# The last layer's output projection: transfers in program order, four weight blocks in other buffers, and weight blocks scaled one block earlier

## The chip, the cores and the metric

The kernel runs on one core of a Trainium2 chip. TensorE (PE; its weight loads are shown as PEld), VectorE (DVE), ScalarE (ACT) and GpSimd (POOL) each work through their own instructions in order; SyncE (SP) here only issues transfers (DMA). The metric is the device time of one execution in microseconds (us), as the median of several runs.

## The reference

One inference step of an encoder trunk of two layers, with D = 1024, on 512 prompt tokens and 32 sample tokens, 544 columns in all. In each layer

```python
h = rmsnorm(x, norm_w)
mix, qm, gate = split(h @ w_in)
out = concat([mixer(mix), mem_attention(qm)]) * silu(gate)     # 2048 wide
x = x + out @ w_out                                            # 2048 x 1024
```

Layer 0's mixer is RWKV-7. Layer 1's is differential attention with 12 heads: for each head two softmaxes over two halves of 64 of the keys, one subtracted from the other with a factor, times the values. A final RMSNorm gives the outputs. Layer 1's keys and values, of prompt and sample, are outputs too. All in fp32; the kernel multiplies operands split in a high and a low part, three products for each pair.

## The kernel before

A class `Trunk` writes out the whole program. Each engine stands behind a `Queue` object: `te` (TensorE), `ve` (VectorE), `ae` (ScalarE), `se` (SyncE's transfers), `ge` (POOL). All their instructions are recorded on one line, L132, so the names of tiles tell them apart in the profile. `tie` (L149) can chain the instructions of a queue in the order in which the program writes them (`self.ordered`); otherwise the framework's scheduler and its waits for buffers set the order on that queue.

*The stream of layer 1* (`stream`). The input projection is 56 weight blocks of 1024x128: for each head its values, keys and queries, then gates and memory queries. A block is 48 matmuls ("steps") of 128x272, 2 halves of the columns, 8 pieces of the inner dimension, 3 products. `h` is the normalized activation in f16, high and low (tiles `hh`, `hl`). While a block is multiplied, other work is laid into its steps by small tables:

- `LOADS1`: two loads of 256 KB bring the fp32 weights of the fourth block ahead into one of four slots (`self.raws`, in the profile `h16s`).
- `STAT1` and `SPREAD1`: ScalarE squares a block three ahead (`junkw`); TensorE totals the squares of a block two ahead (a matmul of 128x1).
- `SCALE1`: VectorE makes a power of two from that total, the scale `s` of the block two ahead (`scales`, `power`).
- `SPLITS1`: the next block is split to f16 tiles `whs`, in six pieces: ScalarE twice writes the high part from the raw weights times `s`, POOL twice multiplies the raw weights by `s` in place (`TENSOR_SCALAR h16s<-h16s`), POOL twice subtracts (`TENSOR_TENSOR whs<-h16s,whs`), which gives the low part.

At the start of each q block the head's keys are split too: ScalarE rounds them (`kh`), POOL takes the low part twice (`kz<-k,kh`), and a transfer `kh<-kh` moves rows. Later steps interleave the head's scores (`ps_s`), softmax and products with the values. At the entry to the stream the first two blocks are measured and scaled at once (`measured`).

*The output projection of layer 1* (`w_out`). 16 blocks of `w_out[1]`, each 1024x128: 8 output columns k, two halves q of the 2048 inputs. Here the operands are fp32r in two parts: `whi` and `wlo` from tiles `raw` (half a block each, `RAWS` = 5 of them), and `hi` and `lo` from the 16 gated branch outputs `og0` to `og15`. The first five blocks are loaded by the end of the stream, by `load_steps` into `raw` tiles, or right after it. The order is (0,0), (1,0), then (0,1), (1,1), then k = 2 to 7; the halves q = 1 use the tiles in the order 12 to 15, 8 to 11. After each block `used` splits the next one and loads another. Split blocks have two buffers each for `whi` and `wlo` and a third pair in a pool `fin` (`self.third`). For each finished half of a column `consume` adds the residual x; from k = 2 it also issues, at the second half of a column (`v.start`), one of six entries of `kv_out`: two transfers that copy keys or values from scratch in DRAM to the outputs (`out_dram<-scr`, 1024 KB and 64 KB). `last` makes the final norm.

SyncE's queue is not tied, so these copies can be issued earlier than the code that writes them stands.

## Time and profile before

| | |
|---|---|
| median of 3 runs | 1378.25 us (1376.0 to 1379.12) |
| profiled execution | 1375.76 us |
| its span in the trace | 1374.0 us |
| mean granted clock of TensorE | 0.987 |
| the stream of layer 1, in the trace | 829 to 1246 us |
| the output projection and the final norm | 1246 to 1374 us |
| busy, TensorE / VectorE / ScalarE / POOL | 95% / 67% / 63% / 46% |

Times in the trace count from the span's start. A row of a timeline gives start, duration, engine, operation, tile written `<-` tiles read, partitions x elements, and in brackets how long the engine was idle before it and which engine's work on which tile ended that idle time. Rows of waits give us in total, number of waits, and the longest.

### The profile page before, as it was taken

Reading aid. Unit: us, or ns where it says so; the run is one execution under the profiler, and the core shown is the slowest. Engines: PE = TensorE matmul, PEld = TensorE weight load, DVE = VectorE, ACT = ScalarE, POOL = GpSimd, SP = SyncE. Lnnn points to the kernel's source line nnn. Section 1 sums busy time; section 2 is a strip of 40 time slices with the busy share of each in tenths; the row PEclk is TensorE's granted clock in tenths of the full one; section 3 lists DMA queues with packets and bytes.
Section 4 is the critical chain, followed back from the end, with each engine's and each line's share of the span. In section 5 each row is a group of like instructions: output and inputs, shape, how many; then the busy total and the mean of one; then the engine's idle time right before and its main releaser. Section 6 shows DMA issues by size and latency. Waiting matters only on the chain. (4 is left out here: it accounts for less than half of the span.)

```text
span 1374.0 us, 32094 instructions
## 1 busy us (share of the span) xinstructions
PE 1304.3 (95%) x11713; PEld 1191.3 (87%) x11713; DVE 923.5 (67%) x2391; ACT 865.0 (63%) x2316; POOL 626.0 (46%) x1103
## 2 busy tenths in 40 slices
PE   6999899999999999899999999999999998998797
PEld 6998799999999999888899997888778887888797
DVE  7776667877787777756674473666796668766343
ACT  7665677677767776655644356777767776773221
POOL 2326675558555855560130037656555655561000
PEclk9999999999999999999999999999999999999899
DMA  7542223322332233224275445777767768766421
GB/s 243 171 135 64 56 66 86 88 72 65 83 89 72 64 83 82 75 78 125 72 234 168 128 143 143 193 164 164 162 155 170 164 140 198 159 155 218 131 70 65
DMA packets 418296, 171.53 MB, mean 125 GB/s; under 512 B 195209, under 2 KB 402578, under 8 KB 418138
## 3 DMA queue, kind: packets, MB, share of 16 engines
q1 hardware_dynamic: 417994, 168.96, 47.3%
q8 instruction: 92, 1.51, 0.5%
q14 instruction: 66, 0.54, 0.1%
q10 hardware_dynamic: 144, 0.52, 0.1%
HBM read 130.84 MB, written 41.92 MB: 126 GB/s over the span
## 5 line engine op out<-in xcount | busy, mean ns | idle before, releaser
L132 PE MATMUL ps_g<-h,whs 128*128 128x272 f16 x2688 | 334.8, 280 | 12.5 <-POOL whs L132 12.5
L132 PEld LDWEIGHTS <-whs 128*128 128x128 f16 x2688 | 254.4, 98 | 67.6 <-POOL whs L132 15.8
L132 PE MATMUL ps_g<-hl,whi 128*128 128x272 f32 x976 | 283.9, 297 | 0.5 <-POOL hl L583 0.5
L132 PE MATMUL ps_g<-hh,wlo 128*128 128x272 f32 x912 | 277.2, 304 | 1.3 <-DVE wlo L132 1.3
L132 PE MATMUL ps_g<-hh,whi 128*128 128x272 f32 x912 | 274.4, 301 | 0.9 <-ACT hh L132 0.9
L872 POOL TENSOR_TENSOR tm<-u,m 102x84 f32<-102x84 f32 (+23 forms) x372 | 155.4, 418 | 164.8 <-DMA m<-sc 134.2
L132 DVE TENSOR_TENSOR wlo<-raw,whi 128x512 fp32r<-128x512 f32 x208 | 149.7, 735 | 83.8 <-ACT whi L132 81.8
L132 ACT CAST whi<-raw 128x512 fp32r<-128x512 f32 x210 | 125.3, 616 | 97.0 <-PE ps_g L132 45.2
L132 PEld LDWEIGHTS ps_g<-hl,whi 128*128 128x128 f32 x976 | 183.7, 190 | 2.4 <-POOL hl L583 0.7
L132 PEld LDWEIGHTS ps_g<-hh,whi 128*128 128x128 f32 x912 | 174.3, 191 | 4.4 <-ACT hh L132 1.3
L132 PEld LDWEIGHTS ps_g<-hh,wlo 128*128 128x128 f32 x912 | 173.9, 191 | 4.7 <-DVE wlo L132 2.1
L874 POOL TENSOR_TENSOR u<-u,tm 102x84 f32<-102x84 f32 (+23 forms) x372 | 161.0, 433 | 29.1
L132 PE MATMUL ps_g<-hi,whi 128*128 128x272 f32 x448 | 130.5, 292 | 10.5 <-ACT hi L132 10.5
L132 POOL TENSOR_SCALAR h16s<-h16s 128x512 f32<-128x512 f32 x112 | 78.9, 716 | 125.6 <-ACT whs L132 118.2
L132 PE MATMUL ps_g<-lo,whi 128*128 128x272 f32 x448 | 130.5, 291 | 0.9 <-DVE lo L132 0.9
L132 PE MATMUL ps_g<-hi,wlo 128*128 128x272 f32 x448 | 130.1, 291 | 0.2 <-DVE wlo L132 0.2
L132 POOL TENSOR_TENSOR whs<-h16s,whs 128x512 f16<-128x512 f32 x112 | 128.7, 1169 | 0.2
L132 PEld LDWEIGHTS ps_g<-hi,whi 128*128 128x128 f32 x448 | 85.4, 191 | 11.0 <-ACT hi L132 10.8
L132 PEld LDWEIGHTS ps_g<-lo,whi 128*128 128x128 f32 x448 | 85.3, 190 | 1.6 <-DVE lo L132 1.6
L132 PEld LDWEIGHTS ps_g<-hi,wlo 128*128 128x128 f32 x448 | 85.3, 190 | 0.4 <-DVE wlo L132 0.4
L132 ACT ACTIVATE whs<-h16s 128x512 f16<-128x512 f32 x112 | 74.9, 715 | 6.0 <-DVE h16s L132 4.8
L132 DVE SCALAR_TENSOR_TENSOR SB<-ps_c,dl,sd 64x64 f32<-64x64 f32 x168 | 47.4, 282 | 44.6 <-PE ps_c L132 40.5
(419 smaller groups left out, 2834.1 us busy)
## 6 DMA issues: line engine op xcount, KB each, us to landing
raw<-in_rw_in_dram SPq DMA_DIRECT2D x114, 256.0 KB
h16s<-in_df_in_dram SPq DMA_DIRECT2D x112, 256.0 KB
raw<-in_w_out_dram SPq DMA_DIRECT2D x64, 256.0 KB
ptr<-pk SPq DMA_DIRECT2D x44, 160.0 KB
aT<-ptr SPq DMA_DIRECT2D x11, 640.0 KB
scr<-sg SPq DMA_DIRECT2D x96, 68.0 KB
out_dram<-scr SPq DMA_DIRECT2D x6, 1024.0 KB
m<-sc SPq DMA_DIRECT2D x36, 128.0 KB
```

What stands on the lines that cost most here:

```text
L132: return lambda *a, **k: self.trunk.tie(self, issue(*a, **k))
L872: nc.gpsimd.tensor_tensor(tm[:, :n, :wd], u3[:, :n, kx : kx + 1].to_broadcast(sh), m3[:, kx : kx + 1, kx + 1 :].to_broadcast(sh), ALU.mult)
L874: nc.gpsimd.tensor_tensor(u3[:, :n, kx + 1 :], u3[:, :n, kx + 1 :], tm[:, :n, :wd], ALU.add)
```

## The change

1. The tables: the split of a block has four pieces (steps 2, 5, 8, 11), not six. POOL's scaling in place goes to a new function `scaled`, called at steps 37 and 41 of the block before the one in which the block is split; the scale itself is made at step 32 (`POWER1`), not 36, and the total at step 12, not 20. ScalarE then copies the scaled weights to f16 and no longer multiplies.
2. From the output projection on, the transfers of SyncE's queue are tied to program order (`self.tied = self.se`), and `used` loads a block only when fewer than two are waiting.
3. The blocks of `w_out[1]` that are loaded during the stream go to the four slots of the stream, not to `raw` tiles, and there are four of them.
4. The third pair of split buffers is one tile `w3` in the space of the f16 activations, which are not read any more then; so the pool that holds them (`hctx`) is closed only at the end.
5. `consume` issues a pair of copies at both halves of the columns 2, 3 and 4.

```diff
-LOADS1, SPLITS1 = (1, 14), (2, 5, 7, 9, 12, 15)
-STAT1, SPREAD1, SCALE1 = (11, 27), 20, 36
+LOADS1, SPLITS1 = (1, 14), (2, 5, 8, 11)
+STAT1, SPREAD1, POWER1, SCALE1 = (14, 27), 12, 32, (37, 41)
...
-        if self.ordered:
+        if self.ordered or self.tied is queue:
...
+    def scaled(self, rec, q):
+
+        x = rec["raw"][:, q * KT // 2 : (q + 1) * KT // 2]
+        self.ge.tensor_scalar(x, x, rec["s"], 1.0, ALU.mult, ALU.mult)
...
             self.scales(rec)
+            for q in range(2):
+                self.scaled(rec, q)
...
-        todo = [(lambda k=k: self.ae.activation(hi[:, k], raw[:, k], AF.Copy, scale=s), 0.0) for k in ks]
-        todo += [(lambda k=k: gp.tensor_scalar(raw[:, k], raw[:, k], s, 1.0, ALU.mult, ALU.mult), 0.0) for k in ks]
+        todo = [(lambda k=k: self.ae.copy(hi[:, k], raw[:, k]), 0.0) for k in ks]
         todo += [(lambda k=k: gp.tensor_tensor(lo[:, k], raw[:, k], hi[:, k], ALU.subtract), 0.0) for k in ks]
...
-        if self.ahead:
+        if self.ahead and (self.tied is None or len(self.early) < 2):
             self.early.append(self.load(*self.ahead.pop(0)))
...
-        p, n = (self.third, 1) if third else (self.wp, 2)
-        hi = p.tile([P, KT, P], F32R, tag="whi", name="whi", bufs=n)
-        lo = p.tile([P, KT, P], F32R, tag="wlo", name="wlo", bufs=n)
+        if third:
+            both = self.third.tile([P, 2, KT, P], F32R, tag="hl", name="w3")
+            hi, lo = both[:, 0], both[:, 1]
+        else:
+            hi, lo = (self.wp.tile([P, KT, P], F32R, tag=x, name=x, bufs=2) for x in ("whi", "wlo"))
...
-            self.hctx.close()
             p = self.pool("fin", 1, ctx=ctx, side="right")
-            self.third, self.turn = p, 2
+            self.third, self.turn, self.tied = self.h0, 2, self.se
...
-                if k >= 2 and v.start and kv_out:
+                if k >= 2 and kv_out:
                     kv_out.pop(0)()
...
-            raws = self.load_steps(*self.ahead.pop(0)) if len(self.early) < (3 if isinstance(self.early[0], dict) else 2) else iter(())
+            raws = self.load_steps(*self.ahead.pop(0)) if len(self.early) < 3 else iter(())
...
-                if i == SCALE1 and self.rec is not None:
+                if i == POWER1 and self.rec is not None:
                     self.scales(self.rec)
+                if i in SCALE1 and self.rec is not None:
+                    self.scaled(self.rec, SCALE1.index(i))
...
+        block = self.raws[self.nscaled % 4]
+        self.nscaled += 1
         for q in range(2):
-            raw = self.wp.tile([P, h, P], F32, tag="raw", name="raw", bufs=RAWS)
-            self.se.dma_start(raw[:], src[q * h * P : (q + 1) * h * P, c0 : c0 + P].rearrange("(k p) c -> p k c", p=P))
+            raw = block[:, q * h : q * h + h]
+            self.se.dma_start(raw, src[q * h * P : (q + 1) * h * P, c0 : c0 + P].rearrange("(k p) c -> p k c", p=P))
```

SyncE's queue at the end of the stream and in the output projection, before (`scr` is scratch in DRAM that holds keys and values, `vt`, `vs` and `aT` belong to the attention):

```order
L132 DMA raw<-in_w_out_dram 128x4x128 x7
L132 DMA out_dram<-scr_12356 512x512
L132 DMA out_dram<-scr_12356 32x512
L132 DMA out_dram<-scr_12357 512x512
L132 DMA out_dram<-scr_12357 32x512
L132 DMA out_dram<-scr_14346 512x512
L132 DMA out_dram<-scr_14346 32x512
L132 DMA out_dram<-scr_14347 512x512
L132 DMA out_dram<-scr_14347 32x512
L132 DMA out_dram<-scr_16419 512x512
L132 DMA out_dram<-scr_16419 32x512
```

The same place after:

```order
L132 DMA h16s<-in_w_out_dram 128x4x128 x6
L132 DMA raw<-in_w_out_dram 128x4x128 x12
L132 DMA out_dram<-scr_12360 512x512
L132 DMA out_dram<-scr_12360 32x512
L132 DMA raw<-in_w_out_dram 128x4x128 x2
L132 DMA out_dram<-scr_12361 512x512
L132 DMA out_dram<-scr_12361 32x512
L132 DMA raw<-in_w_out_dram 128x4x128 x2
L132 DMA out_dram<-scr_14348 512x512
L132 DMA out_dram<-scr_14348 32x512
```

Before, nine half blocks stand ahead of all twelve copies, and the second half of the fifth block behind them, with the other 22 loads; after, twenty half blocks stand ahead of the first copy, and each pair of copies is followed by one block.

POOL's queue around a q block of the first heads, before (`kz` is the low part of the keys; the row of scales behind it belongs to the same block as the row of subtractions behind it):

```order
L132 TENSOR_SCALAR h16s<-h16s 128x512 x2
L132 TENSOR_TENSOR whs<-h16s,whs 128x512 x2
L132 TENSOR_TENSOR kz_12351<-k,kh 64x544 x2
L132 TENSOR_SCALAR h16s<-h16s 128x512 x2
L132 TENSOR_TENSOR whs<-h16s,whs 128x512 x2
```

After:

```order
L132 TENSOR_TENSOR whs<-h16s,whs 128x512 x2
L132 TENSOR_SCALAR h16s<-h16s 128x512 x2
L132 TENSOR_TENSOR kz_12355<-k,kh 64x544 x2
L132 TENSOR_TENSOR whs<-h16s,whs 128x512 x2
L132 TENSOR_SCALAR h16s<-h16s 128x512 x2
```

The scales of the block that is split at the q block have moved from behind `kz` to in front of it; the subtractions follow `kz` directly.

ScalarE's queue at the end of the stream, before (`og_12337` to `og_12340` are the branch outputs 12 to 15, `hi` their high parts, `fw` the final norm's weights):

```order
L132 ACTIVATE osT<-ps_osT,dv 128x128
L132 CAST hi_18532<-og_12337 128x544
L132 CAST hi_18534<-og_12338 128x544
L1830 DMA fw<-in_final_norm_w_dram 128x1024
L132 CAST whi<-raw 128x512 x4
L132 CAST hi_18536<-og_12339 128x544
L132 CAST whi<-raw 128x512
L132 CAST hi_18538<-og_12340 128x544
```

After (`og_12341` to `og_12344` are the branch outputs 12 to 15, `w_18582` is the third buffer):

```order
L132 ACTIVATE osT<-ps_osT,dv 128x128
L132 CAST w_18582<-h16s 128x512 x2
L1837 DMA fw<-in_final_norm_w_dram 128x1024
L132 CAST whi<-h16s 128x512 x2
L132 CAST hi_18526<-og_12341 128x544
L132 CAST hi_18528<-og_12342 128x544
L132 CAST hi_18530<-og_12343 128x544
L132 CAST whi<-raw 128x512 x2
L132 CAST hi_18532<-og_12344 128x544
```

The casts of outputs 12 and 13 now follow two weight blocks, and that of output 15 follows the cast of a whole block from `raw` tiles, where it followed one half block.

## The prediction

> **What bounds the kernel now.** I read the busy times first, then TensorE's waits over the whole run, then the chain of work that ended last in the final stage, and last the two stretches to which these lead.

> ```profile
> span 1374.0 us, 32094 instructions
> PE 1304.3 (95%) x11713; PEld 1191.3 (87%) x11713; DVE 923.5 (67%) x2391; ACT 865.0 (63%) x2316; POOL 626.0 (46%) x1103
> ```

> TensorE (PE) is busy 95% of the span, and no matmul is removed. The kernel can gain only from TensorE's idle time and from time at a lower clock. Four rows of TensorE's waits bear on code that the change touches (us in total, times, longest us):

> ```profile
> PE ps_g L132 <- POOL whs L132: 12.5, 11, 2.3
> PE ps_g L132 <- ACT hi L132: 10.5, 1, 10.5
> PE ps_s L132 <- DMA kh<-kh: 2.0, 1, 2.0
> PE ps_g L132 <- DVE lo L132: 0.9, 2, 0.7
> ```

> The first is the weight stream of layer 1, eleven short waits for the low part of a weight block. The second is one wait in the output projection. The chain in the last stage (start, us, what) says what that one wait really was:

> ```profile
> 1256.59 16.38 DMA out_dram<-scr
> 1273.03 4.97 DMA raw<-in_w_out_dram
> 1278.02 0.73 DVE lo L132
> 1278.80 31.62 PE ps_g L132 x233
> ...
> 1315.14 30.68 PE ps_g L132 x245
> ```

> TensorE waits for activations (`hi`), but the chain goes behind them to a weight load, and behind that to the copies of keys and values to the outputs. ScalarE (ACT), SyncE's queue (SPq) and TensorE at that place:

> ```profile
> 1242.33 6.88 SPq L132 DMA_DIRECT2D raw<-in_w_out_dram  x4
> 1249.26 17.66 SPq L132 DMA_DIRECT2D out_dram<-scr  x12
> 1267.01 65.44 SPq L132 DMA_DIRECT2D raw<-in_w_out_dram  x23
> 1276.76 0.62 ACT L132 CAST whi<-raw 128x512 fp32r<-128x512 f32 x1 [14.42 <-DMA raw<-in_w_out_dram]
> 1277.29 1.73 ACT L132 CAST hi<-og 128x544 fp32r<-128x544 f32 x3
> 1277.98 0.59 PE L132 MATMUL ps_g<-hi,whi 128*128 128x272 f32 x1 [10.54 <-ACT hi L132]
> 1278.80 0.59 PE L132 MATMUL ps_g<-lo,whi 128*128 128x272 f32 x1 [0.22 <-DVE lo L132]
> ```

> All twelve copies are issued in a row, and the load after them is the second half of the fifth weight block. Its cast sits on ScalarE for 14.42 us, and the three casts of `hi` that TensorE needs are queued behind it. Windows (us, busy time and count of PE, PEld, DVE, ACT, POOL, then granted clock, DMA share, GB/s) give the price:

> ```profile
> 1265.00:1285.00 20.00, 9.23 (x53) 8.71 (x52) 4.76 (x8) 4.05 (x8) 0.00 (x0) 0.66 0.70 222
> 1315.00:1345.00 30.00, 30.00 (x242) 30.00 (x241) 10.71 (x20) 7.24 (x14) 0.00 (x0) 1.00 0.16 46
> 1136.90:1140.40 3.50, 3.50 (x20) 2.34 (x19) 3.26 (x10) 2.19 (x9) 2.86 (x3) 0.51 1.04 289
> ```

> In the chain above, 245 matmuls take 30.68 us, 0.1252 each. The 20 us from 1265 hold 53 of them, worth 6.6 us, so 13.4 us are lost: 10.54 + 0.22 of waiting, and 2.6 more, since the granted clock is only 0.66 there.

> [...]

> **The change, part by part.** *Copies and loads in program order.* SyncE now issues four whole blocks in the stream and six more ahead of the first copy; then one pair of copies (1024 and 64 KB), two half loads, and so on. The fifth block no longer stands behind a copy, so the wait of 10.54 us goes, with the 0.22 and the clock loss. Late next is the cast of `hi` for tile 15: it now follows the cast of another weight block on ScalarE, whose buffer TensorE must free. Such a cast takes 0.62 us; I estimate 0.5 us of waiting. The gain is 13.4 − 0.5 = 12.9. Its bounds are 13.4 (no new wait) and 10.0 (the wait is 0.8 and is enough to keep the clock low, 2.6).

> The twelve copies go to output columns 2 to 4, two pairs per column. A column is 96 matmuls, 96 × 0.1252 = 12.0 us. The DMA view of 1249 to 1273 gives what copies cost:

> ```profile
> DMA packets 4747, 7.60 MB, mean 317 GB/s; under 512 B 226, under 2 KB 1487, under 8 KB 4746
> out_dram<-scr SPq DMA_DIRECT2D x6, 1024.0 KB
> out_dram<-scr SPq DMA_DIRECT2D x6, 64.0 KB
> ```

> Two pairs are 2.23 MB, and two weight blocks 1.05 MB; at 317 GB/s that is 7.0 + 3.3 = 10.3 us of the column's 12.0. Before, this stage moves 46 GB/s, so there is room, and a load is issued about a column ahead of its split. Cost: 0, hidden by 12 us of matmuls; if that cover fails it is rival C.

> *POOL's scaling moved to the block before.* At a q block TensorE waits like this (POOL, ScalarE, TensorE):

> ```profile
> 939.85 2.75 POOL L132 TENSOR_TENSOR kz<-k,kh 64x544 fp32r<-64x544 f32 x2 [5.09 <-ACT kh L132]
> 940.59 1.33 ACT L132 ACTIVATE whs<-h16s 128x512 f16<-128x512 f32 x2
> 942.70 1.36 POOL L132 TENSOR_SCALAR h16s<-h16s 128x512 f32<-128x512 f32 x2
> 944.02 2.27 POOL L132 TENSOR_TENSOR whs<-h16s,whs 128x512 f16<-128x512 f32 x2
> 945.23 1.33 PE L132 MATMUL ps_g<-h,whs 128*128 128x272 f16 x10 [0.81 <-POOL whs L132]
> ```

> `kz` holds POOL for 2.75 us, the scale for 1.36, and only then come the subtractions, whose first half TensorE awaits. The high part is ready at 941.92, before `kz` ends, so POOL alone is late. With the scale done in the block before, the subtraction starts right after `kz`, 1.36 us sooner. The eleven waits:

> ```profile
> 829.05 0.64 PE L132 MATMUL ps_g<-h,whs 128*128 128x272 f16 x4 [1.49 <-POOL whs L132]
> 1022.06 1.10 PE L132 MATMUL ps_g<-h,whs 128*128 128x272 f16 x8 [2.28 <-POOL whs L132]
> 1165.73 1.10 PE L132 MATMUL ps_g<-h,whs 128*128 128x272 f16 x8 [1.50 <-POOL whs L132]
> 1211.52 0.87 PE L132 MATMUL ps_g<-h,whs 128*128 128x272 f16 x6 [1.22 <-POOL whs L132]
> ```

> The other seven lie between 0.81 (the row at 945.23) and 1.22. The eight up to 1.22 sum to 12.5 − 1.49 − 2.28 − 1.50 = 7.2 and vanish, since each is under 1.36; 1.50 falls to 0.14 and 2.28 to 0.92, another 2.7. The first (1.49) is the entry to layer 1, where the scales now stand on POOL ahead of the last two splits of the activations; it may grow, by 0.4 as I estimate (half of one scale, 0.7, rounded up). So 7.2 + 2.7 − 0.4 = 9.5.

> Three things take some back. Where VectorE (DVE) is nearly full, TensorE would run into it:

> ```profile
> 981.00:1026.00 45.00, 41.44 (x360) 33.84 (x358) 41.03 (x104) 30.17 (x77) 27.09 (x28) 1.00 0.73 176
> 1018.79 1.11 SPq L132 DMA_DIRECT2D kh<-kh  x2
> 1023.58 0.31 PE L132 MATMUL ps_s<-kh,qp 128*128 128x128 f32 x1
> ```

> VectorE is busy 41.03 of 45 us there, and the waits in this stretch give up about 2.5 of the 9.5; I take 1.5 of it as lost. The scores at 1023.58 need the move of `kh` issued at 1018.79 to 1019.90, so 3.7 us later; scores that come 1.36 sooner may wait for it, as they did elsewhere for 2.0: 0.5. And ScalarE's cast now needs POOL's scale first. That wait is new. Today the order is the other way round:

> ```profile
> L132 POOL TENSOR_SCALAR h16s<-h16s 128x512 f32<-128x512 f32 x112 | 78.9, 716 | 125.6 <-ACT whs L132 118.2
> L132 ACT ACTIVATE whs<-h16s 128x512 f16<-128x512 f32 x112 | 74.9, 715 | 6.0 <-DVE h16s L132 4.8
> ```

> POOL idles 118.2 us in front of its scales, so it has room to do them sooner, at steps 37 and 41 of the block before, where no cast is pending. ScalarE's cast follows at steps 2 and 5, some thirteen matmuls after the first scale. If the scale is still behind something, the cast waits at most one scale, 0.72 us. Bounds: 0 if never, 12 × 0.72 = 8.6 if in each of the twelve q blocks and if TensorE feels all of it; nearest is the row of 6.0 us, ScalarE's waits today in front of these casts, nearly all off TensorE's path: 0.5. The stream gains 9.5 − 1.5 − 0.5 − 0.5 = 7.0, with bounds of 0.9 (9.5 − 8.6) and 12.5 (all of the row).

> *Edits at no cost.* The total of squares (a 128x1 matmul pair) moves from step 20 to 12, within the same TensorE work. The third split buffer moves to the space of the activations, free when the stream's last matmul ends. The cast without a scale operand has the same size. The gate on loads (fewer than two waiting) only spaces them; the 12 us column covers it.

> **Sum.** 12.9 + 7.0 = 19.9. Against the profiled execution of 1375.76 us that gives 1355.9; its span of 1374.0 lies 1.8 lower. The median of the runs, 1378.25, is 2.5 above that execution, so for the median I say 1378.25 − 19.9 = 1358.3, rounded to 1358.

> **Rivals.** *A, both parts work:* 1358, by the bounds of small costs 1352 (25.9 gained, every wait gone) to 1362.

> *B, only the output projection pays:* the stream's waits come back as waits for VectorE, for `kh` or for POOL's scale. For it speaks VectorE at 41.03 of 45 us; against it that most of the eleven waits end on POOL with the high part long ready. 1378.25 − 12.9 = 1365.

> *C, the copies now delay the weights:* copies and loads share SyncE's queue, so each column's loads run behind two pairs of copies. At the 222 GB/s of the window from 1265, 3.28 MB need 14.8 us, 2.8 more than a column. Three columns are 8.4, and three clock drops at about 1.7 (half of the 3.5 us at 0.51) 5.1: the 13.5 undo the output part, 1378.25 − 7.0 + 0.6 ≈ 1372. It decides below 3.28 MB / 12.0 us = 273 GB/s. Against it: 317 was measured with the same copies, and the lead of a column is 12 us.

> [...]

> *D, slower:* the new wait of ScalarE for POOL's scale. ScalarE works in order, so a cast that waits holds the exponentials and evacuations behind it, which TensorE needs. If it cost 0.72 us in each of the 56 blocks it would be 40: 1378.25 − 19.9 + 40 ≈ 1398. It decides from 19.9 / 0.72 = 28 blocks on. Against it: POOL has those 118.2 us of idling.

> That the change does not reorder the transfers is excluded by SyncE's order of instructions.

> **Chances.** A 0.64, B 0.20, C 0.09, D 0.04; 0.03 for gains lost in waits that I do not see. The predicted time is A's. The range reaches from A's best, 1351 with the spread of the runs, over B's 1365 and half way to C: 1351 to 1370. Faster by over 0.2% (2.75 us, about what a measurement of this kernel can tell from no change) are A, B and C: 0.93; the same 0.03; slower 0.04.

> **What would show it.** In the changed profile: no wait of TensorE for `hi` of more than 1 us near 1267, a granted clock of 1 through the output projection, copies spread over columns 2 to 4 with loads of `raw` between them and no wait of TensorE for `whi` or `wlo` there; TensorE's waits for POOL `whs` down from 12.5 to about 3 us; POOL's 118.2 us of waiting for ScalarE gone, and in its place waits of ScalarE's `whs` for POOL `h16s`, small. It would be wrong if those last are many and long (D), if new waits on `ps_s` appear beside `kh` or VectorE (B), or if `raw` lands late in columns 3 to 5 (C).

## The result, and the profile after

The changed kernel takes 1358.47 us (median of 4 runs, 1353.73 to 1360.9), the kernel before 1378.68 (4 runs) on the same chip: a ratio of 0.9852, 95% interval 0.9819 to 0.9884, so 20 us less (16 to 25). Forecast were 1358 and 19.9 us less. The sum was right; one of its terms was not, as the runs below show.

The profiled execution is the slowest of the four, 1360.9 us. Its page begins:

```profile
span 1359.1 us, 32016 instructions
PE 1304.9 (96%) x11713; PEld 1192.7 (88%) x11713; DVE 922.2 (68%) x2391; ACT 856.3 (63%) x2316; POOL 630.8 (46%) x1103
```

TensorE does the same work in a span 14.9 us shorter; this is less than the 20 us of the medians because the execution profiled before, of 1375.76 us, was faster than the four runs compared here, and this one is the slowest of its four. Of its waits over the whole run, these are in the code that was changed:

```profile
PE ps_g L132 <- POOL whs L132: 3.6, 2, 2.9
PE ps_s L132 <- DMA kh<-kh: 2.9, 2, 2.2
...
PE ps_mo L132 <- DVE og L132: 1.4, 2, 1.0
PE ps_s L132 <- DVE og L132: 1.3, 1, 1.3
PE ps_aT L132 <- DVE pt L132: 1.3, 1, 1.3
...
PE ps_o L132 <- DMA aT<-ptr: 0.6, 1, 0.6
```

The wait of 10.5 us for `hi` is gone. The eleven waits for POOL have become two. In their place stand short waits for VectorE, for `kh` and for `aT`, of which the kernel before had one for `kh`, of 2.0 us, and one for VectorE, of 0.2 us. In front of its scales POOL no longer waits for ScalarE, 118.2 us before, but for VectorE, which makes the scale:

```profile
L132 POOL TENSOR_SCALAR h16s<-h16s 128x512 f32<-128x512 f32 x112 | 79.1, 719 | 89.0 <-DVE h16s L132 83.0 <-PE ps_o L132 2.1 <-PE ps_g L132 2.0
```

The queues of SyncE and of ScalarE in the output projection:

```profile
1231.00 48.31 SPq L132 DMA_DIRECT2D raw<-in_w_out_dram  x12
1279.35 1.25 SPq L132 DMA_DIRECT2D out_dram<-scr  x2
1280.71 4.66 SPq L132 DMA_DIRECT2D raw<-in_w_out_dram  x2
1285.42 1.18 SPq L132 DMA_DIRECT2D out_dram<-scr  x2
...
1256.56 1.15 ACT L132 CAST whi<-h16s 128x512 fp32r<-128x512 f32 x2 [8.33 <-PE ps_g L132]
1257.60 1.74 ACT L132 CAST hi<-og 128x544 fp32r<-128x544 f32 x3
1259.52 1.15 ACT L132 CAST whi<-raw 128x512 fp32r<-128x512 f32 x2 [0.18 <-PE ps_g L132]
1260.57 2.84 ACT L132 CAST hi<-og 128x544 fp32r<-128x544 f32 x5
```

Copies now come in pairs, 6 to 8 us apart. The weight cast in front of output 15 waits only 0.18 us for a buffer, and output 15 itself (the first of the five casts at 1260.57) is done ahead of its matmuls, so the 0.5 us that the forecast put there are not felt. Two windows (us, busy time and count of PE, PEld, DVE, ACT, POOL, granted clock, DMA share, GB/s): the first is the one in which 13.4 us were lost before, the second holds the copies.

```profile
1265.00:1285.00 20.00, 20.00 (x162) 20.00 (x161) 8.26 (x17) 6.54 (x14) 0.00 (x0) 1.00 0.42 130
1279.00:1315.00 36.00, 36.00 (x291) 35.85 (x291) 15.19 (x28) 8.00 (x16) 0.00 (x0) 1.00 0.77 251
```

From the last matmul of the stream to the end it was 127.8 us before (1246.20 to 1374.04) and is 114.0 now (1245.14 to 1359.09): 13.9 of the 14.9 us. The stream, from its first to its last matmul, went from 419.0 to 416.6 in this execution, only 2.4 shorter where 7.0 were forecast; what stands ahead of the stream was 1.4 longer in it. That gap is what most of the runs are about.

### The profile page after: what moved, and what is told of

It is laid out like the page before. It is cut to its first block, busy times and chain, and to the rows that moved or that the text cites. A ratio compares the mean times of both kernels' runs of the same rounds, so it can differ in the third digit from the quotient of the medians.

```text
span 1359.1 us, 32016 instructions
## 1 busy us (share of the span) xinstructions
PE 1304.9 (96%) x11713; PEld 1192.7 (88%) x11713; DVE 922.2 (68%) x2391; ACT 856.3 (63%) x2316; POOL 630.8 (46%) x1103
## 5 line engine op out<-in xcount | busy, mean ns | idle before, releaser
L132 PE MATMUL ps_g<-h,whs 128*128 128x272 f16 x2688 | 334.1, 281 | 3.6 <-POOL whs L132 3.6
L132 PEld LDWEIGHTS <-whs 128*128 128x128 f16 x2688 | 256.9, 98 | 57.7 <-POOL whs L132 5.3
L132 PE MATMUL ps_g<-hl,whi 128*128 128x272 f32 x960 | 281.5, 298 | 0.6 <-POOL hl L591 0.5
L132 PE MATMUL ps_g<-hh,wlo 128*128 128x272 f32 x912 | 277.9, 305 | 1.3 <-DVE wlo L132 1.3
L132 PE MATMUL ps_g<-hh,whi 128*128 128x272 f32 x912 | 275.1, 302 | 0.9 <-ACT hh L132 0.9
L132 DVE TENSOR_TENSOR wlo<-raw,whi 128x512 fp32r<-128x512 f32 x194 | 140.8, 739 | 64.6 <-ACT whi L132 63.4
L132 PEld LDWEIGHTS ps_g<-hl,whi 128*128 128x128 f32 x960 | 181.6, 191 | 2.4 <-POOL hl L591 0.7
L132 PEld LDWEIGHTS ps_g<-hh,whi 128*128 128x128 f32 x912 | 174.8, 192 | 4.4 <-ACT hh L132 1.3
L132 PEld LDWEIGHTS ps_g<-hh,wlo 128*128 128x128 f32 x912 | 174.3, 191 | 4.8 <-DVE wlo L132 2.1
L132 POOL TENSOR_TENSOR whs<-h16s,whs 128x512 f16<-128x512 f32 x112 | 130.7, 1187 | 51.4 <-ACT whs L132 49.7
L132 ACT CAST whi<-raw 128x512 fp32r<-128x512 f32 x194 | 116.2, 616 | 58.1 <-PE ps_g L132 31.0
L132 POOL TENSOR_SCALAR h16s<-h16s 128x512 f32<-128x512 f32 x112 | 79.1, 719 | 89.0 <-DVE h16s L132 83.0
L132 PE MATMUL ps_g<-hi,whi 128*128 128x272 f32 x384 | 110.7, 288 | 0.9 <-ACT whi L132 0.9
L132 PE MATMUL ps_g<-lo,whi 128*128 128x272 f32 x384 | 110.7, 288 | 0.7 <-DVE lo L132 0.7
L132 PE MATMUL ps_g<-hi,wlo 128*128 128x272 f32 x384 | 110.6, 288 | 0.2 <-DVE wlo L132 0.2
L132 DVE SCALAR_TENSOR_TENSOR SB<-ps_c,dl,sd 64x64 f32<-64x64 f32 x168 | 47.4, 282 | 43.5 <-PE ps_c L132 39.1
L132 PEld LDWEIGHTS ps_g<-hi,whi 128*128 128x128 f32 x384 | 72.2, 188 | 1.2 <-ACT whi L132 1.2
L132 PEld LDWEIGHTS ps_g<-lo,whi 128*128 128x128 f32 x384 | 72.2, 188 | 1.1 <-DVE lo L132 1.1
L132 PEld LDWEIGHTS ps_g<-hi,wlo 128*128 128x128 f32 x384 | 72.3, 188 | 0.4 <-DVE wlo L132 0.4
L132 ACT CAST whs<-h16s 128x512 f16<-128x512 f32 x112 | 65.4, 619 | 9.5 <-POOL h16s L132 7.7
## 6 DMA issues: line engine op xcount, KB each, us to landing
out_dram<-scr SPq DMA_DIRECT2D x6, 1024.0 KB
```

What stands on the lines that cost most here:

```text
L132: return lambda *a, **k: self.trunk.tie(self, issue(*a, **k))
```

## The experiments

Ratios are against the kernel before on the same chip in the same session, whose medians were 1374.3 to 1375.4 us.

**Each part alone.** The first run keeps the old tables, `split_scaled` and `measured`, the second the old output projection.

> The output projection's part alone (transfers in program order, four blocks in the stream's slots, copies two pairs a column); the splits of the stream stand as before. If the two parts add: 12.9 to 13.9 us under before, about 1365, no wait of TensorE for hi near 1267, its waits for POOL whs still about 12.5 us. Rival (the stream's part brings nothing, the rest of the 20 us is in the output projection too): about 1359.

Measured: 0.9897 (0.9873 to 0.9920), 1361.1 us, 13.2 under before.

> The stream's part alone (POOL's scale one block earlier); the output projection as before, so the wait of 10.5 us for hi stays. By the prediction 7.0 us under before, about 1371.5. Rival, from one profiled execution of the changed kernel, whose stream is only 2.4 us shorter (waits for POOL whs 8.9 us less, but 4.9 of other waits and one half-clock stretch at the entry more): about 1376, not to be told from before.

Measured: 0.9961 (0.9945 to 0.9977), 1369.6 us, 4.7 under before. TensorE's waits, in the output part alone and then in the stream's part alone:

```profile
PE ps_g L132 <- POOL whs L132: 12.7, 11, 2.3
PE ps_s L132 <- DMA kh<-kh: 2.3, 2, 2.1
```

```profile
PE ps_g L132 <- ACT hi L132: 10.2, 1, 10.2
PE ps_g L132 <- POOL whs L132: 3.6, 2, 2.9
PE ps_s L132 <- DMA kh<-kh: 2.8, 3, 1.5
PE ps_mo L132 <- DVE og L132: 1.4, 2, 1.0
PE ps_aT L132 <- DVE pt L132: 1.3, 1, 1.3
```

Each part removes its own wait and leaves the other's. They add within the scatter: 1.03% and 0.39% make 1.42%, against 1.48% and, in a second measurement, 1.42% for both; by medians 13.2 and 4.7 make 17.9 us, against 20.2 and 19.2. In the trace of the stream's part the stream takes 413.0 us, 6.0 less than before, and its waits sum to 9.1 us against 15.1: the same 6.0, with one half clock in each (a granted clock of 0.79 from 829 to 837 in the part alone, of 0.51 from 1136.90 to 1140.40 before). So waits explain that trace. The stream differs from one execution to the next: with the changed tables of steps it took 416.6, 413.0, 413.0, 412.1 and 415.9 us in five traces, 414.1 on average, against an average of 419.4 in the four traces with the old tables. That is 5.3 us less.

**What removes the stall: program order or more blocks ahead?** One run takes program order away from the changed kernel, one gives it alone to the kernel before, one drops the copies from the kernel before (four outputs are then not written).

```diff
-        if self.ordered or self.tied is queue:
+        if self.ordered:
```

> The changed kernel without program order on SyncE's queue; four blocks in the stream's slots, the gate on loads and two pairs a column stay in the code, but all twelve copies are again issued in a row, now behind 13 half blocks instead of 9. Theory (program order is what takes the stall away): the 14th half block lands late and TensorE waits some 5 us or more, 1365 or above. Rival (it is enough that more blocks are ahead of the copies): a block is 48 matmuls, 6.0 us, so the seventh is needed 36 us after the stage begins, about 1281 in the trace; the copies have landed by about 1273 and the load 5 us later, so no wait over 1 us and a time within 2 us of the changed kernel.

```diff
-        if self.ordered:
+        if self.ordered or self.tied is queue:
...
-            self.third, self.turn = p, 2
+            self.third, self.turn, self.tied = p, 2, self.se
```

> The kernel before with one thing of the change: SyncE's transfers in program order from the output projection on (no more blocks in the stream, no third buffer moved, copies at the second half of a column, stream as before). All loads of the first ten blocks then stand ahead of the copies. Theory (any order that takes the loads of the fifth to seventh block out from behind the copies does): the 10.5 us for hi are gone, 10 to 13 us under before, unless the last copies, now among the final stores, end later than the norm. Rival (the four blocks in the stream's slots are needed): a wait of several us stays near 1267.

```diff
-                if k >= 2 and v.start and kv_out:
-                    kv_out.pop(0)()
```

> The kernel before without the twelve copies of keys and values, so these four outputs aren't written. Theory (the stall is the copies in front of a load): the wait for hi is gone and so is the half clock, 13 us under before. Rival (the buffers are what is late, for which the copies only fill the time): the wait stays above 3 us.

Measured: 0.9848 (0.9824 to 0.9873) without program order, as the whole change; 0.9888 (0.9869 to 0.9906) with program order alone, as the output part alone; 0.9899 (0.9877 to 0.9921) without copies, the same again. SyncE's queue without program order, then with program order alone:

```profile
1226.20 3.12 SPq L132 DMA_DIRECT2D raw<-in_w_out_dram  x5
1229.37 14.66 SPq L132 DMA_DIRECT2D out_dram<-scr  x12
1256.26 56.59 SPq L132 DMA_DIRECT2D raw<-in_w_out_dram  x19
```

```profile
1239.60 44.07 SPq L132 DMA_DIRECT2D raw<-in_w_out_dram  x17
1283.72 1.26 SPq L132 DMA_DIRECT2D out_dram<-scr  x2
```

In the first, all copies are again in a row in front of nineteen loads, and nothing waits: six and a half blocks are ahead of them. The copies were the cause of the stall, and either half of the cure is enough. How many blocks must stand ahead of the copies was not tried between four and a half, which stall, and six and a half, which do not.

**What do the copies cost now?** The changed kernel without them (the same four outputs not written).

> The changed kernel without the twelve copies of keys and values, so these four outputs aren't written. Theory (a column's 12.0 us hide two pairs of copies and two blocks): the same time as the changed kernel within 1 us, 0.985 of before. Rival (copies still delay weights or the final stores): 2 us or more under the changed kernel, 0.983 or less.

Measured: 0.9856 (0.9837 to 0.9876), against 0.9858 (0.9839 to 0.9878) of the changed kernel in its second measurement, below. They cost nothing that these runs can tell, whose intervals reach some 2.7 us to either side.

**The entry to the stream.** The first wait for POOL grew from 1.49 to 2.86 us. TensorE and POOL there, in the changed kernel:

```profile
831.78 0.64 PE L132 MATMUL ps_g<-h,whs 128*128 128x272 f16 x3 [2.86 <-POOL whs L132]
...
822.77 1.79 POOL L132 TENSOR_SCALAR h16s<-h16s 128x512 f32<-128x512 f32 x2
824.53 1.66 POOL L1753 TENSOR_TENSOR h<-hn,h 128x544 f16<-128x544 f32 x1
826.17 1.36 POOL L132 TENSOR_SCALAR h16s<-h16s 128x512 f32<-128x512 f32 x2
827.51 1.22 POOL L1753 TENSOR_TENSOR h<-hn,h 128x544 f16<-128x544 f32 x1
```

Two blocks are scaled in front of the last two splits of the activations `h`, and POOL has been working without a pause since 821. In the first run below VectorE scales the first block and POOL the second only behind the first block's split, which leaves the second block's split unscaled, so it tells of the wait and is no version to use; in the next VectorE scales both, and POOL the third.

```diff
-            for q in range(2):
-                self.scaled(rec, q)
+            if rec["n"] < 2:                # first run: == 0
+                self.ve.tensor_scalar(rec["raw"], rec["raw"], rec["s"], None, ALU.mult)
+            else:
+                self.pend.append(rec)       # scaled by POOL in stream, behind the first block's split
...
```

> The changed kernel, but at the entry to layer 1 VectorE scales the first block, and POOL scales the second only after the first block's split, so that no scale stands ahead of the last two splits of the activations on POOL. Theory: the first wait, 2.86 us in the changed kernel against 1.49 before, falls to 1.5 or less, and the half clock behind it (3.4 us, worth 1.7) goes: 3 us under the changed kernel, about 1355.5. Rival (the scales aren't what POOL is late with): the wait stays over 2.5 and the time about 1358.5.

> As in the run on the entry, with both first blocks scaled by VectorE and the third by POOL after the first split. Theory: as there, no wait for POOL whs at the first block and no half clock behind it, 3 us under the changed kernel, 0.982 of before. Rival (the time in that run came from the late scale of the second block): the wait comes back and 0.985 of before.

Measured: 0.9841 (0.9815 to 0.9866) and 0.9833 (0.9809 to 0.9857). In the second the only wait for POOL left is the one inside a q block:

```profile
PE ps_s L132 <- DMA kh<-kh: 1.6, 2, 1.0
PE ps_o L132 <- DMA aT<-ptr: 1.5, 1, 1.5
...
PE ps_st L132 <- ACT junkw L132: 0.9, 2, 0.4
...
PE ps_g L132 <- POOL whs L132: 0.7, 1, 0.7
```

The wait at the entry and the half clock behind it are gone (from 829 to 837 the granted clock is 1.00, where the changed kernel has 0.79), and the stream takes 410.6 and 409.5 us. A part of that is only moved: two waits for ScalarE's squares (`junkw`), 0.9 us in all, now stand just ahead of the stream's first matmul, where the changed kernel has none. So scales ahead of the splits of `h` were what made POOL late. By medians the second is 1351.3 us; that it beats the changed kernel is likely from the trace, but the intervals overlap.

**The slower rival.**

```diff
-STAT1, SPREAD1, POWER1, SCALE1 = (14, 27), 12, 32, (37, 41)
+STAT1, SPREAD1, POWER1, SCALE1 = (14, 27), 12, 36, (45, 46)
```

> The changed kernel with the power of two at step 36 and POOL's scales at steps 45 and 46 instead of 37 and 41, so that ScalarE's casts at steps 2 and 5 follow closely. For the slower rival of the prediction (the new wait of ScalarE for POOL): ScalarE's waits for POOL h16s, 7.7 us in the changed kernel, go to 20 us or more, and if TensorE feels them the kernel is 5 us or more over the changed one. Theory (TensorE does not feel waits of ScalarE under a scale's 0.72 us, since a block has 7 us of slack in ScalarE's work): the waits grow, the time stays within 2.5 us of the changed kernel.

Measured: 0.9862 (0.9842 to 0.9881), the time of the changed kernel. ScalarE's waits for the scale, in the changed kernel and in this one:

```profile
ACT whs L132 <- POOL h16s L132: 7.7, 11, 2.6
```

```profile
ACT whs L132 <- POOL h16s L132: 10.7, 9, 3.3
```

They grow by 3.0 us, not to the 20 that the rival named, and TensorE does not feel them. The 7 us of slack in the expectation are no idle time of ScalarE, which in the changed kernel is busy 289 of the 417 us from 829 to 1246, some 2.3 us idle for each of the 56 blocks; they are about one block's length, by which the splits run ahead. The intervals leave room for some 2.7 us either way. So the margin is not that narrow; how late the scale must be to cost time was not found.

**Moving `kh` off SyncE's queue**, tried for a faster version, on the kernel with both first blocks scaled by VectorE:

```diff
-                self.se.dma_start(st["kh"][rows[1 - m], m, :].bitcast(F32), ...)
+                self.ae.dma_start(st["kh"][rows[1 - m], m, :].bitcast(F32), ...)
```

> As the run with both first blocks scaled by VectorE, and the 24 moves of kh are issued by ScalarE, not on SyncE's queue, where the one at 1130.34 in the changed kernel stands behind four stores and a load. Theory (scores wait for kh because SyncE issues it late): the waits of ps_s for kh, 2.9 us in the changed kernel, and the half clock that sometimes follows near 1135 go, 1 to 4 us under that run, 0.981 of before. Rival (24 issues of some 0.4 us on ScalarE and their waits push back its exponentials): no gain, or 2 us more.

Measured: 1.0015 (1.0002 to 1.0029), 1377.9 us, some 25 us over the same kernel with `kh` on SyncE (0.9833). Neither theory said that much. The scores' waits for `kh` are indeed gone; but TensorE's and SyncE's waits have these rows:

```profile
PE ps_o L132 <- DMA aT<-ptr: 22.9, 8, 6.0
...
SPq L132 <- DMA kh<-kh: 49.5, 13, 5.7
```

SyncE now stops thirteen times until a move of `kh`, issued by ScalarE, has landed, and `aT`, which the products with the values need, is issued late. ScalarE's exponentials (`pt`) are not what fell behind: TensorE waits 0.7 us for them in all. In the traces of the kernels before and after, the landings of all transfers are counted on eight semaphores, some 2080 to 2160 landings on each; and with `kh` on SyncE's own queue, in the run with both first blocks scaled by VectorE, SyncE's waits in the stream have no row for `kh`. That the moves hold up SyncE because both queues share these semaphores is my reading and was not shown; a version with a semaphore of their own was not tried.

**The changed kernel once more, and the last candidate.**

> The changed kernel unchanged, on the chip of the next run, for a second trace of it. If its first trace was typical, the stream is again 416 to 417 us and its waits 11 us; if that trace had a stray wait and a stray half clock, as the stream's part alone (413.0) suggests, about 413, the wait of 2.9 us at the entry and the half clock behind it stay, and the time is 0.985 of before.

> Both first blocks scaled by VectorE, four blocks in the stream's slots, and no program order on SyncE's queue. Theory (program order changes nothing once four blocks are in the slots, and the entry is worth 3 us): 3 us under the changed kernel on this chip, 0.983 of before. Rival (the entry's gain is within the scatter): the same as the changed kernel.

Measured: 0.9858 (0.9839 to 0.9878), 1356.2 us, and 0.9842 (0.9818 to 0.9866), 1354.0 us. Of the two cases in the expectation for the changed kernel the first held: its stream took 415.9, not about 413, again with a half clock at the entry (a granted clock of 0.79 from 829 to 837). The candidate's stream took 410.7, and its median is 2.2 us under the changed kernel's on the same chip, where 3 were expected; the intervals overlap, so that gain is not shown in time. Without program order it is no slower than the run with it (0.9833), as far as the intervals tell.

## Why the prediction was right, and where not

**The output projection, 12.9 forecast.** The trace gives 13.9, the part alone 13.2 by medians and 14.2 by the ratio. The chain of causes (copies, load, cast, `hi`) was the right one; dropping the copies alone gives the same. The 2.6 of clock came back with the wait: from 1265 to 1285 the granted clock is 1.00, where it was 0.66. The 0.5 for the cast of output 15 did not come.

**The copies, 0 forecast.** 0: with and without them 0.9858 and 0.9856. Rival C is out; in the window from 1279 TensorE never pauses.

**The stream, 7.0 forecast; that part alone gave 4.7 by medians, 5.4 by the ratio (3.2 to 7.6) and 6.0 in its trace.** The main term held: of ten waits inside q blocks, 11.0 us before, one of 0.73 is left, and it is the one of 2.28 for which 0.92 was forecast. The step that failed is the entry: "it may grow, by 0.4 as I estimate". It grew by 1.37, and in the changed kernel a half clock of 3.4 us followed, worth 1.7 more by my estimate, half of its length. From 829 to 837 the granted clock is 0.79 in both traces of the changed kernel and in that of the stream's part alone; in the run without copies, which has the wait too, it stayed at 1.00. So that term was up to 3.1, not 0.4. (In the trace of the part alone the granted clock over the stream's 413.0 us rounds to 1.00, which leaves room for the half clock at the entry, 0.996 by my estimate, but not for a second one near 1137, 0.992; that paid the 1.7 back. In the changed kernel's first trace it stayed, 0.50 from 1135.84.) The forecast counted half a scale where two scales stood ahead of the last but one split of `h` and four ahead of the last. The offsets were of about the right kind: in the trace of the part alone VectorE cost 2.7 us where 1.5 was taken (4.0 in the changed kernel's first trace), and `kh` and `aT` 0.8 (1.5 there) where 0.5 was; ScalarE's wait for POOL cost nothing that TensorE feels where 0.5 was. So of rival B a part is true.

**The sum.** By the traces of the parts the output projection gave 1.0 us more than forecast and the stream 1.0 less, so the misses cancel. The gain itself is known only to lie between 16 and 25 us, and was 19.2 the second time. That the forecast lies within a microsecond of the measured time is therefore partly luck. Two bounds of the prediction do not follow from its terms: gains of 10.0 and 0.9 would put the slow end of A at 1367, not 1362, and half way from B's 1365 to C's 1372 is 1368.5, not 1370.

**Program order.** The forecast said that the fifth block is no longer behind a copy, and took program order as the means. That alone does it, but the four blocks in the stream's slots do it as well.

## What to carry to other kernels

When a chain of waits ends in a transfer, ask which single transfer is late and what is queued ahead of it; a few loads placed earlier may be all that is needed, and two cures for one wait do not add. When work is moved to an earlier place on an engine, price every place to which it goes: here the twelve q blocks were counted with care and the entry, where the moved scales stand in front of splits that TensorE awaits, was given a guess. And a transfer moved to another engine's queue can make the first queue wait for it, here 49.5 us in thirteen waits.

## What the runs showed of the hardware

```profile
828.64:832.05 3.41, 0.55 (x6) 0.23 (x4) 0.37 (x2) 1.38 (x4) 3.30 (x6) 1.00 0.01 2
832.05:835.47 3.42, 3.42 (x18) 2.46 (x16) 0.00 (x0) 0.00 (x0) 3.31 (x6) 0.50 0.62 176
1132.43:1135.84 3.41, 1.50 (x13) 1.31 (x14) 1.00 (x6) 2.46 (x8) 2.01 (x2) 1.00 0.86 148
1135.84:1139.25 3.41, 3.41 (x17) 2.28 (x16) 2.99 (x17) 1.59 (x7) 0.55 (x2) 0.50 1.07 302
```

```profile
825.78:829.19 3.41, 2.19 (x20) 1.84 (x19) 0.53 (x3) 3.08 (x9) 3.30 (x6) 1.00 0.00 0
829.19:832.61 3.42, 1.80 (x16) 1.58 (x17) 0.00 (x0) 0.00 (x0) 3.36 (x5) 1.00 0.18 51
832.61:836.02 3.41, 3.41 (x32) 2.87 (x30) 0.00 (x0) 0.76 (x2) 3.36 (x5) 1.00 0.64 182
```

The window in which TensorE idles 2.86 of 3.41 us, and the one with 1.91, are each followed by one at half clock. The same wait at the entry, 2.8 us, falls across two windows in the run without copies, 1.2 in one and 1.6 in the next, and the clock stays at 1.00. In the kernel before, the wait of 2.0 us for `kh` lies within one window (1133.54 to 1136.95), and the granted clock of the next is 0.50; the wait of 2.28 us at 1022 lies across two, 1.12 in one and 1.16 in the next, and the clock stays at 1.00 there too. From 820 us on, in the traces before and after, all six windows at full clock with 1.91 us idle or more were followed by half clock, and none of those with 1.49 or less. Ahead of 820 that count does not hold: there half clock also followed windows with 0.06 us idle, two in each trace. So a wait of 2 to 3 us at these places was followed by half clock where it fell into one window of the grid, and was not where it fell across two; I estimate such a half clock at 1.7 us, half of 3.41. It may be a part of the scatter between runs of one kernel; that was not tried.
